# Hybrid five-branch layer: TensorE kept in program order throughout, and the merge of branch D put ahead of that of branch B

## The chip, the cores and the metric

The kernel runs on one core of one Trainium2 chip. The metric is the time on the device in microseconds (us), from which a median over several runs is taken. Each run of the profiler also leaves one traced execution, and all durations below come from that one.

## The reference

One layer over 256 tokens of width 1024. One large projection feeds five branches that read the same input: A causal block attention, B a mixture of three dilated windows, C attention with forgetting, D a gated delta rule, E cross-attention into a memory of 256 tokens. Each branch's output is gated, projected back to width 1024, weighted by a sigmoid gate and summed.

```
h = x @ w_in + b_in                       # every q, k, v, z and merge gate
o_a, o_b, o_c, o_d, o_e                   # 256 x 384 each, 6 heads of 64 (E: 4 of 96)
o = stack(o_a .. o_e) * silu(z)           # (S, 5, 384)
y = einsum('snc,ncd->snd', o, w_branch)   # 5 projections to width 1024
y = sum(sigmoid(merge_logits) * y, axis=n)
return layer_norm(2**0.25 * x + y @ w_out)
```

D needs small serial pieces: a causal convolution of 4 taps on its q, k and v, cumulative sums of log decays, and a triangular solve in chunks of 64.

## The kernel before

**Main stream.** Every large product is made of units. A unit loads 128x1024 of weights (`raw`, 7 buffers), ScalarE rounds them to `hi` and VectorE takes the rest `lo` (helper `split`; 3 buffers each), and TensorE then runs three matmuls for each block of 128 (`mm3`: hi by hi, hi by lo, lo by hi), 24 matmuls of 256 columns for a feature-major unit. `ORDER` is the list of blocks, three or four units each: `dk` is D's key projection, `zc` the gate of C, `merge_b` the merge of branch B (8 times 24 matmuls for the gate and 9 for the projection). A merge block needs its branch's gated output and calls `need("og" + br)` before its projection.

**Side streams.** The branches' own work is written as generators (`scalars`, the convolutions `conv`, `d_front`, `d_base`, `d_levels`, `d_solve`, three `attend`, `cross`, and so on). After each chunk of a unit (9 matmuls as a rule) `stepper` lets up to three of them take a step. In a step a generator issues a few instructions and yields, one or more chunks. All logits of all branches go through one PSUM tile (`lg`, one buffer, helper `lgps`), transposes through two (`tp`), the outputs of the heads through one (`av`).

**What sets the order on an engine.** The program is only the first word on it. The framework's scheduler plays the program against a timeline of its own at compile time and sets a fixed order for each engine; an instruction that is not ready there is passed by others that are. `tc.keep_in_program_order(ins)` takes an instruction out of that freedom with respect to the others marked so. Before, only the last out-projections carry the mark (`keep=not first`). On the chip each engine follows its fixed list.

Names in the lists below: `mm_299`, `mm_370` and `mm_417` are the PSUM tiles of successive units (second and third unit of `dk`, first of `dq`), `fg` the log decays that `scalars` makes from a chain of some twenty small VectorE instructions (L333 to L360), `tp_353` and `tp_357` their cumulative sums (L364 to L369), `grow` a copy of those that goes to DRAM (`gscr`, L376) and comes back broadcast as `gr` (L465, for D) and `mf` (L797, for C; L802 and L803 turn it into masks), `yc` the convolution (L389 to L392), `dconv` its result (L397), which L432 (q and k) and L451 (v) transpose. `lg_4595` and `lg_4599` are logits of the cross-attention (L897), whose exponentials L905 makes before L911 transposes them. L738 to L767 are the softmax of A, B and C (L754 the exponentials on ScalarE), L773 its transposes and L776 their copy, L689 the gating.

Of the kernel before, what the change touches and what calls it, by code (L numbers as in the profile page):

```python
# [29 lines left out]
ORDER = ("dk dq cq dv ck zc av za ak zd aq bq0 bk0 bk2 bq1 merge_a bk1 bv"  # L30
         " merge_c zb bq2 ze eq mk mv merge_b merge_d merge_e").split()
MERGES = [n for n in ORDER if n.startswith("merge")]
# [43 lines left out]
def kernel(ctx: ExitStack, tc: tile.TileContext, T: dict, out: bass.AP):  # L76
# [8 lines left out]

    V_, A_, PE, G_ = nc.vector, nc.scalar, nc.tensor, nc.gpsimd
    uid = [0]

# [36 lines left out]

    def mm3(pt, lh, ll, rh, rl, first, last, keep=False):
        for l, r, start, stop in ((lh, rh, first, False), (lh, rl, False, False), (ll, rh, False, last)):
            ins = PE.matmul(pt, l, r, start=start, stop=stop)  # L128
            if keep:
                tc.keep_in_program_order(ins)  # L130

    def together(*products):

        for pt, l, r, start, stop in products:
            PE.matmul(pt, l, r, start=start, stop=stop)  # L135

# [174 lines left out]
    for _ in range(WARM):  # L311
        PE.matmul(wup[:, 0], zero[:, 0:P], zero, start=True, stop=True)

    def scalars():

        yield from wait("sc")
        nc.sync.dma_start(cst[:, C_MA:], T["cst"][:, C_MA:])
        nc.sync.dma_start(gnw, T["gnw"])
        nc.sync.dma_start(mgb, T["mgb"])
        nc.sync.dma_start(vb, T["vb"].to_broadcast([P, 2, BW]))  # L320

        V_.tensor_scalar(cwh, cw, 0.5, None, op0=ALU.mult)
        hb = bcol[:, 3 * len(FM):]
        V_.tensor_scalar(hb, hb, 0.5, None, op0=ALU.mult)
# [36 lines left out]
        yield  # L361

        pt = tpps((P, 2, 18))
        PE.matmul(pt[:, 0], K(C_TRI), fg[:, 0], start=True, stop=True)  # L364
        PE.matmul(pt[:, 1], K(C_ONE), fg[:, 0], start=True, stop=False)
        PE.matmul(pt[:, 1], K(C_TRI), fg[:, 1], start=False, stop=True)
        p2 = tpps((18, S))
        PE.matmul(p2, fg[:, 0], K(C_TRI, 256), start=True, stop=False)
        PE.matmul(p2[:, P:], fg[:, 1], K(C_TRI), start=False, stop=True)  # L369
        yield  # L370
        V_.tensor_scalar(ngt, pt, -1.0, None, op0=ALU.mult)
        grow = ct("grow", (18, S))
        V_.tensor_copy(grow, p2)
        R["gscr"] = dr.tile([18, S], F32, name="gscr")
        yield
        nc.sync.dma_start(R["gscr"], grow)  # L376
        flag("scalars")
# [45 lines left out]
    def d_front():  # L423
# [3 lines left out]
        for qi, key in ((1, "k"), (0, "q")):  # L427
            yield from wait((key, 2))
            for t in range(2):
                pt = tpps((P, 3, P))  # L430
                for m in range(3):
                    PE.transpose(pt[:, m], dconv[key][:, m, t * P:(t + 1) * P], ident)  # L432
                yield
# [14 lines left out]
        for t in range(2):  # L448
            pt = tpps((P, 6, HD))
            for m in range(3):  # L450
                PE.transpose(pt[:, 2 * m:2 * m + 2], dconv["v"][:, m, t * P:(t + 1) * P], ident)  # L451
            yield
# [103 lines left out]
    def d_levels():  # L556
# [5 lines left out]
        for b in range(4):  # L562
            r = slice(32 * b, 32 * b + 32)
            for g in range(12):
                PE.matmul(y[r, g], AT[r, g, r], Tc[r, g, 0:16], start=True, stop=True)
            yield
# [4 lines left out]
        for b in range(4):  # L571
            r, c = slice(32 * b, 32 * b + 32), 32 * (b % 2)
            for g in range(12):
                PE.matmul(z[32 * b:32 * b + 16, g], ys[r, g, 0:16], Uc[r, g, c + 16:c + 32], start=True, stop=True)
                if b % 2 == 0:
                    PE.matmul(zt[r, g], Uc[r, g, 0:32], ys[r, g, 0:16], start=True, stop=True)
            yield
# [9 lines left out]
        for i, j in ab:  # L587
            for g in range(12):
                PE.matmul(y[j, g], AT[i, g, j], Tc[i, g], start=True, stop=True)
            yield  # L590
# [5 lines left out]
        for i, j in ab:  # L596
            for g in range(12):
                PE.matmul(z[i, g], ys[j, g], Uc[j, g, 32:64], start=True, stop=True)
            yield
# [5 lines left out]
    def d_solve():  # L605
# [5 lines left out]
        def solve(g):  # L611
            hs, hsl = range(3 * g, 3 * g + 3), slice(3 * g, 3 * g + 3)
            for t in range(2):
                if t == 1:
                    pt = tpps((P, 3, HD))
                    for x, h in enumerate(hs):
                        PE.matmul(pt[:, x], AT[:, 12 + h], W[:, 0, h], start=True, stop=True)
                    yield
                    V_.tensor_tensor(V[:, 1, hsl], V[:, 1, hsl], pt, op=ALU.subtract)
                    yield  # L620
                for b in range(2):
                    r = slice(64 * b, 64 * b + 64)
                    if b == 1:
                        pt = tpps((P, 3, HD))
                        for x, h in enumerate(hs):
                            PE.matmul(pt[r, x], AT[0:64, 6 * t + h, r], W[0:64, t, h], start=True, stop=True)
                        yield
# [3 lines left out]
                    for x, h in enumerate(hs):  # L631
                        PE.matmul(pt[r, x], Uc[r, 6 * t + h], V[r, t, h], start=True, stop=True)
                    yield
# [10 lines left out]
        for t in range(2):  # L644
            pt = lg[:, t]
            for h in range(H):
                if t == 0:
                    PE.matmul(pt[:, h], PT[:, h], W[:, 0, h], start=True, stop=True)
                else:
                    PE.matmul(pt[:, h], PT[:, 12 + h], W[:, 0, h], start=True, stop=False)  # L650
                    PE.matmul(pt[:, h], PT[:, 6 + h], W[:, 1, h], start=False, stop=True)
                if h % 2:
# [65 lines left out]
    def attend(br, groups, vname, maskf, width):  # L718
# [5 lines left out]
        def pair(m):  # L724
# [46 lines left out]
            for x in range(2):  # L771
                for i in range(3):
                    PE.transpose(lg[:, x, i * P:(i + 1) * P], L[x][0][:, i * P:(i + 1) * P], ident)  # L773
            yield
# [41 lines left out]
    def mem_norm():  # L816
# [25 lines left out]
        for k in range(KD):  # L842
            pt = tpps((P, S))
            for t in range(2):
                PE.transpose(pt[:, t * P:(t + 1) * P], mr[t][:, k * P:(k + 1) * P], ident)
            yield
# [23 lines left out]
    def token_gate(o, zs, br, scalar=None):  # L870
        dst = R["og" + br] = (f3t(F32R), f3t(F32R))
        for m in range(3):
            pt = tpps((P, S))
            for t in range(2):
                PE.transpose(pt[:, t * P:(t + 1) * P], o[:, t, m * P:(m + 1) * P], ident)
            yield
# [5 lines left out]
    def cross():  # L882
# [5 lines left out]
        def pair(t, g):  # L888
# [4 lines left out]
            for x, h in enumerate(hs):  # L893
                parts = HQ[h]
                for i, (m, a0, a1) in enumerate(parts):
                    krhs = kp if (h == 3) else ke[:, m]
                    PE.matmul(lg[:, x, :S], qe[a0:a1, m, t * P:(t + 1) * P], krhs[a0:a1], start=i == 0, stop=i == len(parts) - 1)  # L897
            yield
# [10 lines left out]
            for pe, pt in zip(pes, (p2[:, 0], p2[:, 1])):  # L909
                for x in range(2):  # L910
                    PE.transpose(pt[:, x], pe[:, x * P:(x + 1) * P], ident)  # L911
            yield
# [5 lines left out]
            for i, h in enumerate(hs):  # L918
                for x in range(2):
                    PE.matmul(avt[t][:, h], pT[:, i, x], ve[:, x, h * 96:(h + 1) * 96], start=x == 0, stop=x == 1)  # L920
            if g == 1:
# [75 lines left out]
    def out_units():  # L997
# [3 lines left out]
        def out_mm(u, k, t, i, first, last):  # L1001
# [5 lines left out]
            else:  # L1007
                h, l = u.h[:, lo:hi], u.l[:, lo:hi]
            mm3(fin["p"][t][i][:, :hi - lo], yh, yl, h, l, first, last, keep=not first)

# [171 lines left out]
```

## Time and profile before

| | |
|---|---|
| median of 3 runs | 498.63 us (498.0 to 501.67) |
| the profiled execution | 500.0 us |
| its span, first to last instruction | 497.9 us |
| TensorE busy | 475.3 us, 95% of the span |
| VectorE busy | 338.1 us, 68% |
| ScalarE busy | 270.3 us, 54% |
| mean granted TensorE clock | 0.964 of full speed |

The time of the profiled execution is 2.1 us more than its span. PE stands for TensorE, DVE for VectorE, ACT for ScalarE, POOL for GpSimd, SP for the queue that issues the loads. A granted clock of 1.00 is 2.4 GHz, 0.50 is 1.2 GHz.

### The profile page before, as it was taken

How to read it: one execution, taken by the hardware profiler on the slowest of the kernel's cores; microseconds unless marked ns; L12 is line 12 of the kernel's file. 1: busy time of each engine (PE TensorE's matmuls, PEld its weight loads, DVE VectorE, ACT ScalarE, POOL GpSimd, SP SyncE). 2: the span in 40 equal slices, each digit the busy share in tenths (PEclk: the TensorE clock that was granted, in tenths of full speed). 3: DMA queues.
4: the chain of work that ended last, by engine and by line, in shares of the span. 5: the costliest groups of instructions: out<-in, count | busy, mean ns of one | idle time of the engine just before them, and what ended most of it. 6: DMA issues, size and time to landing. Idle time of an engine off the chain costs nothing. (4 is left out here: it accounts for less than half of the span.)

```text
span 497.9 us, 10146 instructions
## 1 busy us (share of the span) xinstructions
PE 475.3 (95%) x3957; PEld 442.7 (89%) x3957; DVE 338.1 (68%) x764; ACT 270.3 (54%) x521; POOL 30.7 (6%) x36
## 2 busy tenths in 40 slices
PE   7999999989989999999999999999969999999994
PEld 4999999979978999999999999898737999999973
DVE  4898998876955344669886664866543766678747
ACT  5555684765654233386645566737364555467610
POOL 0000030120000000000001110000001212100000
PEclk9999999999999599999999999999958999999997
DMA  8995676453533123356566874534600566677302
GB/s 262 363 334 179 205 232 216 153 167 102 170 70 109 57 59 118 117 151 189 176 192 200 257 229 139 155 102 127 240 35 0 176 190 183 202 224 232 141 1 84
DMA packets 35052, 81.38 MB, mean 163 GB/s; under 512 B 8971, under 2 KB 17469, under 8 KB 34877
## 3 DMA queue, kind: packets, MB, share of 16 engines
q1 hardware_dynamic: 34715, 80.22, 51.3%
q8 instruction: 31, 0.51, 0.4%
q10 hardware_dynamic: 288, 0.52, 0.3%
q14 instruction: 18, 0.13, 0.1%
HBM read 79.37 MB, written 1.36 MB: 162 GB/s over the span
## 5 line engine op out<-in xcount | busy, mean ns | idle before, releaser
L124 DVE TENSOR_TENSOR lo<-raw,hi 128x1024 fp32r<-128x1024 f32 (+4 forms) x163 | 172.5, 1060 | 88.8 <-ACT hi L123 88.2
L123 ACT ACTIVATE hi<-raw 128x1024 fp32r<-128x1024 f32 (+4 forms) x163 | 146.4, 901 | 139.6 <-PE mm L128 102.8
L128 PE MATMUL mm<-xhi,hi 128*128 128x256 f32 x776 | 221.1, 285 | 0.2
L128 PE MATMUL mm<-xhi,lo 128*128 128x256 f32 x776 | 219.0, 283 | 0.7 <-DVE lo L124 0.7
L128 PE MATMUL mm<-xlo,hi 128*128 128x256 f32 x776 | 218.5, 282 | 0.0
L128 PEld LDWEIGHTS mm<-xhi,lo 128*128 128x128 f32 x776 | 147.7, 191 | 4.1 <-issue 1.4
L128 PEld LDWEIGHTS mm<-xhi,hi 128*128 128x128 f32 x776 | 148.1, 191 | 2.8 <-issue 1.0
L128 PEld LDWEIGHTS mm<-xlo,hi 128*128 128x128 f32 x776 | 148.2, 191 | 0.6 <-issue 0.3
L128 PE MATMUL mm<-f,hi 128*128 128x256 f32 x240 | 45.3, 283 | 0.1
L972 POOL TENSOR_TENSOR yacc<-yacc,yt 128x256 f32<-128x256 f32 x24 | 20.0, 838 | 312.1 <-DVE yt L971 312.1
L128 PEld LDWEIGHTS mm<-f,hi 128*128 128x128 f32 x240 | 36.8, 188 | 1.0 <-ACT f L123 0.5
L128 PE MATMUL mm<-f,lo 128*128 128x256 f32 x120 | 33.7, 282 | 0.0
L128 PEld LDWEIGHTS mm<-f,lo 128*128 128x128 f32 x120 | 22.6, 188 | 0.1
L954 ACT ACTIVATE th<-mm,bcol 128x256 f32<-128x256 f32 x40 | 18.3, 458 | 0.0
L128 PE MATMUL mm<-hi,xhi 128*128 128x384 f32 (+1 forms) x48 | 16.5, 367 | 2.0 <-ACT hi L123 2.0
L128 PE MATMUL mm<-lo,xhi 128*128 128x384 f32 (+1 forms) x48 | 17.5, 364 | 0.4 <-DVE lo L124 0.4
L754 ACT ACTIVATE pr<-pr,mm 128x128 f32<-128x128 f32 (+1 forms) x36 | 15.8, 443 | 3.6 <-DVE mm L745 3.6
L128 PE MATMUL mm<-hi,xlo 128*128 128x384 f32 (+1 forms) x48 | 17.1, 357 | 0.0
L738 DVE CUSTOM_DVE_ANT_0 pr<-lg,cst 128x128 f32<-128x128 f32 (+1 forms) x48 | 14.4, 352 | 4.0 <-PE lg L135 4.0
L135 PE MATMUL lg<-f,f 64*128 64x256 f32 (+1 forms) x144 | 16.9, 351 | 0.0
L971 DVE SCALAR_TENSOR_TENSOR yt<-th,mm 128x256 f32<-128x256 f32 x32 | 13.4, 420 | 3.7 <-PE mm L128 2.8
L480 POOL TENSOR_SCALAR_AFFINE_SELECT pr<-pr 128x256 f32<-128x256 f32 x6 | 9.4, 1576 | 95.3 <-DVE pr L479 91.3
(234 smaller groups left out, 577.1 us busy)
## 6 DMA issues: line engine op xcount, KB each, us to landing
raw<-in_wf_dram SPq DMA_DIRECT2D x60, 512.0 KB, 4.3
raw<-in_wm_dram SPq DMA_DIRECT2D x40, 512.0 KB, 3.7
raw<-in_wb_dram SPq DMA_DIRECT2D x40, 192.0 KB, 2.4
raw<-in_wt_dram SPq DMA_DIRECT2D x12, 384.0 KB, 3.5
raw<-in_wo_dram SPq DMA_DIRECT2D x8, 512.0 KB, 4.7
gr<-gscr SPq DMA_DIRECT2D x12, 128.0 KB, 3.4
raw<-in_wcs_dram SPq DMA_DIRECT2D x3, 402.0 KB, 6.5
raw<-in_mem_dram SPq DMA_DIRECT2D x2, 512.0 KB, 3.4
```

The source lines that it names most:

```text
L123: A_.activation(hi, src, AF.Copy)
L124: V_.tensor_tensor(lo, src, hi.bitcast(F32), op=ALU.subtract)
L128: ins = PE.matmul(pt, l, r, start=start, stop=stop)
L135: PE.matmul(pt, l, r, start=start, stop=stop)
L480: G_.affine_select(E[:, 0::2], E[:, 0::2], pattern=[[0, 2], [1, P]], compare_op=ALU.is_ge, fill=-BIG, base=0, channel_multiplier=-1)
L738: V_.tensor_tensor_reduce(l[:, sl], pts[x][:, sl], mk[x][:, sl], 1.0, 3.0e38, ALU.add, ALU.min, mx[x][:, t, g:g + 1])
L754: A_.activation(l[:, sl], l[:, sl], AF.Exp, bias=mms[x][:, t:t + 1], scale=-1.0, accum_out=sm_[x][:, t, g:g + 1])
L954: A_.activation(th, p, AF.Tanh, bias=bcol[:, i:i + 1], scale=0.5)
L971: V_.scalar_tensor_tensor(yt, st_["th"], 1.0, st_["p"], op0=ALU.add, op1=ALU.mult)
L972: (V_ if last else G_).tensor_tensor(yacc[:, d], yacc[:, d], yt, op=ALU.add)
```

## The change

Two things. The mark that keeps program order is put on every TensorE instruction of the kernel (each matmul and each transpose), so that the scheduler can't move any of them past another. And in `ORDER` the block `merge_d` changes places with `merge_b`. VectorE, ScalarE, GpSimd and the loads are still ordered by the scheduler, which now plays them against a TensorE that waits where its next instruction waits.

```diff
-         " merge_c zb bq2 ze eq mk mv merge_b merge_d merge_e").split()
+         " merge_c zb bq2 ze eq mk mv merge_d merge_b merge_e").split()
...
+    keep = tc.keep_in_program_order
...
-    def mm3(pt, lh, ll, rh, rl, first, last, keep=False):
+    def mm3(pt, lh, ll, rh, rl, first, last):
         for l, r, start, stop in ((lh, rh, first, False), (lh, rl, False, False), (ll, rh, False, last)):
-            ins = PE.matmul(pt, l, r, start=start, stop=stop)
-            if keep:
-                tc.keep_in_program_order(ins)
+            keep(PE.matmul(pt, l, r, start=start, stop=stop))
...
-            PE.matmul(pt, l, r, start=start, stop=stop)
+            keep(PE.matmul(pt, l, r, start=start, stop=stop))
...
-        PE.matmul(pt[:, 0], K(C_TRI), fg[:, 0], start=True, stop=True)
+        keep(PE.matmul(pt[:, 0], K(C_TRI), fg[:, 0], start=True, stop=True))
...
-                    PE.transpose(pt[:, m], dconv[key][:, m, t * P:(t + 1) * P], ident)
+                    keep(PE.transpose(pt[:, m], dconv[key][:, m, t * P:(t + 1) * P], ident))
...
-            mm3(fin["p"][t][i][:, :hi - lo], yh, yl, h, l, first, last, keep=not first)
+            mm3(fin["p"][t][i][:, :hi - lo], yh, yl, h, l, first, last)
```

Line numbers: the change moves the lines from 88 to 125 of the kernel before down by two; from 132 on they agree again.

TensorE's list, third and fourth unit. Before, the second unit of `dk` is followed by the next units:

```order
L128 MATMUL mm_299<-xhi,hi_226 128x256
L128 MATMUL mm_299<-xlo,hi_226 128x256
L128 MATMUL mm_299<-xhi,lo_227 128x256
L128 MATMUL mm_370<-xhi,hi_295 128x256
L128 MATMUL mm_370<-xlo,hi_295 128x256
L128 MATMUL mm_417<-xhi,hi_366 128x256
L128 MATMUL mm_417<-xlo,hi_366 128x256
L128 MATMUL mm_370<-xhi,lo_296 128x256
```

In the changed kernel the cumulative sums of `scalars` stand there:

```order
L130 MATMUL mm_299<-xhi,hi_226 128x256
L130 MATMUL mm_299<-xlo,hi_226 128x256
L130 MATMUL mm_299<-xhi,lo_227 128x256
L364 MATMUL tp_353<-fg,cst 128x18
L365 MATMUL tp_353<-fg,cst 128x18
L366 MATMUL tp_353<-fg,cst 128x18
L368 MATMUL tp_357<-cst,fg 18x256
L369 MATMUL tp_357<-cst,fg 18x128
L130 MATMUL mm_370<-xhi,hi_295 128x256
L130 MATMUL mm_370<-xlo,hi_295 128x256
L130 MATMUL mm_370<-xhi,lo_296 128x256
```

The five products of L364 to L369 have moved from the eleventh unit to between the second and the third, ahead of some 200 matmuls of the main stream.

VectorE's list at the same place. Before, the chain that makes `fg` runs in between the splits and the convolution (`lo_461` is the weight rest for the sixth unit of `dk` and `dq`):

```order
L347 TENSOR_TENSOR s_269<-s_269,e 128x24
L407 MEMSET xp_455 128x3
L392 SCALAR_TENSOR_TENSOR yc_384<-xp_361,cwh,yc_384 128x256
L348 TENSOR_TENSOR s_270<-s_269 128x24
L124 TENSOR_TENSOR lo_461<-raw_293,hi_460 128x1024
L407 MEMSET xp_506 128x3
L349 TENSOR_SCALAR lp<-s_270 128x24
L397 SCALAR_TENSOR_TENSOR f_29_289<-th_345,yc_323 128x256
```

In the changed kernel the chain is finished first, and the masks of C follow it at once:

```order
L359 TENSOR_SCALAR fg<-lp 128x6 x2
L360 TENSOR_TENSOR fg<-lp,fg 128x6 x2
L371 TENSOR_SCALAR ngt<-tp_353 128x36
L373 COPY grow<-tp_357 18x256
L802 SCALAR_TENSOR_TENSOR mf_1101<-mf_1101,ngt,cst 128x128
L803 SCALAR_TENSOR_TENSOR mf_1101<-mf_1101,ngt,cst 128x256
L802 SCALAR_TENSOR_TENSOR mf_1102<-mf_1102,ngt,cst 128x128
L126 TENSOR_TENSOR lo_461<-raw_293,hi_460 128x1024
L389 TENSOR_SCALAR yc_427<-xp_408,cwh 128x256
```

`lo_461` has moved from amid the chain to behind the rest of it and behind three instructions that read `mf`, which comes back from DRAM after L373.

TensorE's list where the cross-attention begins. Before, it stands in a projection of `merge_b` (`f_651` and `f_652` are the two parts of B's gated output, `mm_4882` the projection):

```order
L128 MATMUL mm_4882<-f_651_3895,hi_4836 128x256
L128 MATMUL mm_4882<-f_652_3896,hi_4836 128x256
L128 MATMUL mm_4882<-f_651_3895,lo_4837 128x256
L897 MATMUL lg_4595<-f_734_4347,f_705_4199 128x256 x3
L911 MATMUL tp_4650<-cst,pr_4631 128x128 x2
L897 MATMUL lg_4599<-f_734_4347,f_705_4199 128x256 x2
L897 MATMUL lg_4599<-kp_4442,f_705_4199 128x256
L911 MATMUL tp_4650<-cst,pr_4633 128x128 x2
L920 MATMUL av_4678<-f_779_4572,pT_4663 128x96 x4
```

In the changed kernel it stands in the first unit of `merge_d`, with main matmuls behind it:

```order
L130 MATMUL mm_4581<-xhi,lo_4551 128x256
L897 MATMUL lg_4595<-f_734_4347,f_705_4199 128x256 x3
L897 MATMUL lg_4599<-f_734_4347,f_705_4199 128x256 x2
L897 MATMUL lg_4599<-kp_4442,f_705_4199 128x256
L130 MATMUL mm_4581<-xhi,hi_4550 128x256
L130 MATMUL mm_4581<-xlo,hi_4550 128x256
```

The first transposes (L911), which stood between the two sets of logits, have moved behind 24 main matmuls, and the second set follows the first directly.

## Rows read from the trace of the kernel before

**Rows 1.** The page: busy time by engine, and the clock in 40 slices.

```profile
PE 475.3 (95%) x3957; PEld 442.7 (89%) x3957; DVE 338.1 (68%) x764; ACT 270.3 (54%) x521; POOL 30.7 (6%) x36
...
PEclk9999999999999599999999999999958999999997
```

**Rows 2.** Stretches: busy time and count by engine, granted clock, DMA share, GB/s.

```profile
24.40:64.90 40.50, 40.50 (x343) 39.31 (x342) 37.13 (x99) 24.12 (x44) 0.87 (x2) 1.00 0.71 235
64.90:104.90 40.00, 40.00 (x316) 37.68 (x314) 35.62 (x89) 26.30 (x52) 8.26 (x4) 1.00 0.58 191
104.90:140.00 35.10, 33.33 (x288) 30.11 (x287) 27.12 (x89) 22.00 (x46) 1.32 (x3) 1.00 0.49 143
140.00:158.00 18.00, 16.11 (x206) 14.36 (x205) 8.05 (x25) 8.84 (x22) 0.00 (x0) 0.91 0.44 118
158.00:175.00 17.00, 17.00 (x203) 15.68 (x199) 7.33 (x18) 5.95 (x14) 0.00 (x0) 0.70 0.13 43
175.00:310.00 135.00, 135.00 (x1228) 131.52 (x1227) 86.18 (x159) 73.87 (x126) 6.81 (x8) 1.00 0.56 168
310.00:354.00 44.00, 42.74 (x331) 38.41 (x329) 28.66 (x80) 28.39 (x67) 0.00 (x0) 1.00 0.48 159
354.00:390.00 36.00, 29.85 (x166) 22.39 (x167) 17.51 (x48) 17.44 (x56) 3.42 (x3) 0.81 0.16 52
```

**Rows 3.** Chain that ended last, in order of time: start us, us, what.

```profile
360.77 5.36 ACT pr L754 x24
366.13 0.46 ACT pr L905 x2
...
366.64 0.69 PE tp L911 x2
```

**Rows 4.** TensorE's timeline: first matmuls of two units (48 apart), and L364 to L369.

```profile
24.10 0.28 PE L128 MATMUL mm<-xhi,hi 128*128 128x256 f32 x1
...
29.76 0.28 PE L128 MATMUL mm<-xhi,hi 128*128 128x256 f32 x1
...
48.72 0.26 PE L364 MATMUL tp<-fg,cst 128*128 128x18 f32 x1
...
49.80 0.38 PE L369 MATMUL tp<-cst,fg 128*18 128x128 f32 x2
```

**Rows 5.** VectorE's timeline: the third split, the chain of `scalars`, the copy, the mask.

```profile
25.33 1.23 DVE L124 TENSOR_TENSOR lo<-raw,hi 128x1024 fp32r<-128x1024 f32 x1 [0.74 <-ACT hi L123]
...
29.04 0.18 DVE L348 TENSOR_TENSOR s<-s 128x24 f32<-128x24 f32 x1
...
45.23 0.23 DVE L360 TENSOR_TENSOR fg<-lp,fg 128x6 f32<-128x6 f32 x2
...
50.85 0.41 DVE L373 COPY grow<-tp 18x256 f32<-18x256 f32 x1
...
60.43 0.34 DVE L802 SCALAR_TENSOR_TENSOR mf<-mf,ngt,cst 128x128 f32<-128x128 f32 x1
```

**Rows 6.** The queue of loads (SP): issue of `grow` to DRAM and of its two readers.

```profile
51.28 0.36 SPq L376 DMA_DIRECT2D gscr<-grow  x1
53.57 2.04 SPq L465 DMA_DIRECT2D gr<-gscr  x4
...
56.13 1.86 SPq L797 DMA_DIRECT2D mf<-gscr  x4
```

**Rows 7.** Groups by line and shape: count, busy us, mean ns, idle before.

```profile
L124 DVE TENSOR_TENSOR lo<-raw,hi 128x1024 fp32r<-128x1024 f32 x106 | 134.7, 1272 | 56.8 <-ACT hi L123 56.2 <-PE mm L128 0.2
...
L392 DVE SCALAR_TENSOR_TENSOR yc<-xp,cwh,yc 128x256 f32<-128x256 f32 x18 | 8.3, 476 | 0.1
...
L776 ACT ACTIVATE pT<-lg 128x768 f32<-128x768 f32 x9 | 7.3, 808 | 13.2 <-PE lg L773 13.1
...
L500 DVE SCALAR_TENSOR_TENSOR big<-lg,cj,pr 128x256 f32<-128x256 f32 x12 | 5.7, 477 | 0.0
...
L738 DVE CUSTOM_DVE_ANT_0 pr<-lg,mf 128x256 f32<-128x256 f32 x6 | 2.5, 419 | 0.0
```

More of the change, by code (lines that the diff above doesn't have):

```diff
@@ L311 @@
     for _ in range(WARM):
-        PE.matmul(wup[:, 0], zero[:, 0:P], zero, start=True, stop=True)
+        keep(PE.matmul(wup[:, 0], zero[:, 0:P], zero, start=True, stop=True))
     def scalars():
@@ L363, in scalars @@
         pt = tpps((P, 2, 18))
-        PE.matmul(pt[:, 0], K(C_TRI), fg[:, 0], start=True, stop=True)
-        PE.matmul(pt[:, 1], K(C_ONE), fg[:, 0], start=True, stop=False)
-        PE.matmul(pt[:, 1], K(C_TRI), fg[:, 1], start=False, stop=True)
+        keep(PE.matmul(pt[:, 0], K(C_TRI), fg[:, 0], start=True, stop=True))
+        keep(PE.matmul(pt[:, 1], K(C_ONE), fg[:, 0], start=True, stop=False))
+        keep(PE.matmul(pt[:, 1], K(C_TRI), fg[:, 1], start=False, stop=True))
         p2 = tpps((18, S))
-        PE.matmul(p2, fg[:, 0], K(C_TRI, 256), start=True, stop=False)
-        PE.matmul(p2[:, P:], fg[:, 1], K(C_TRI), start=False, stop=True)
+        keep(PE.matmul(p2, fg[:, 0], K(C_TRI, 256), start=True, stop=False))
+        keep(PE.matmul(p2[:, P:], fg[:, 1], K(C_TRI), start=False, stop=True))
         yield
@@ L450, in d_front @@
             for m in range(3):
-                PE.transpose(pt[:, 2 * m:2 * m + 2], dconv["v"][:, m, t * P:(t + 1) * P], ident)
+                keep(PE.transpose(pt[:, 2 * m:2 * m + 2], dconv["v"][:, m, t * P:(t + 1) * P], ident))
             yield
@@ L564, in d_levels @@
             for g in range(12):
-                PE.matmul(y[r, g], AT[r, g, r], Tc[r, g, 0:16], start=True, stop=True)
+                keep(PE.matmul(y[r, g], AT[r, g, r], Tc[r, g, 0:16], start=True, stop=True))
             yield
@@ L573, in d_levels @@
             for g in range(12):
-                PE.matmul(z[32 * b:32 * b + 16, g], ys[r, g, 0:16], Uc[r, g, c + 16:c + 32], start=True, stop=True)
+                keep(PE.matmul(z[32 * b:32 * b + 16, g], ys[r, g, 0:16], Uc[r, g, c + 16:c + 32], start=True, stop=True))
                 if b % 2 == 0:
-                    PE.matmul(zt[r, g], Uc[r, g, 0:32], ys[r, g, 0:16], start=True, stop=True)
+                    keep(PE.matmul(zt[r, g], Uc[r, g, 0:32], ys[r, g, 0:16], start=True, stop=True))
             yield
@@ L588, in d_levels @@
             for g in range(12):
-                PE.matmul(y[j, g], AT[i, g, j], Tc[i, g], start=True, stop=True)
+                keep(PE.matmul(y[j, g], AT[i, g, j], Tc[i, g], start=True, stop=True))
             yield
@@ L597, in d_levels @@
             for g in range(12):
-                PE.matmul(z[i, g], ys[j, g], Uc[j, g, 32:64], start=True, stop=True)
+                keep(PE.matmul(z[i, g], ys[j, g], Uc[j, g, 32:64], start=True, stop=True))
             yield
@@ L616, in solve @@
                     for x, h in enumerate(hs):
-                        PE.matmul(pt[:, x], AT[:, 12 + h], W[:, 0, h], start=True, stop=True)
+                        keep(PE.matmul(pt[:, x], AT[:, 12 + h], W[:, 0, h], start=True, stop=True))
                     yield
@@ L625, in solve @@
                         for x, h in enumerate(hs):
-                            PE.matmul(pt[r, x], AT[0:64, 6 * t + h, r], W[0:64, t, h], start=True, stop=True)
+                            keep(PE.matmul(pt[r, x], AT[0:64, 6 * t + h, r], W[0:64, t, h], start=True, stop=True))
                         yield
@@ L631, in solve @@
                     for x, h in enumerate(hs):
-                        PE.matmul(pt[r, x], Uc[r, 6 * t + h], V[r, t, h], start=True, stop=True)
+                        keep(PE.matmul(pt[r, x], Uc[r, 6 * t + h], V[r, t, h], start=True, stop=True))
                     yield
@@ L647, in d_solve @@
                 if t == 0:
-                    PE.matmul(pt[:, h], PT[:, h], W[:, 0, h], start=True, stop=True)
+                    keep(PE.matmul(pt[:, h], PT[:, h], W[:, 0, h], start=True, stop=True))
                 else:
-                    PE.matmul(pt[:, h], PT[:, 12 + h], W[:, 0, h], start=True, stop=False)
-                    PE.matmul(pt[:, h], PT[:, 6 + h], W[:, 1, h], start=False, stop=True)
+                    keep(PE.matmul(pt[:, h], PT[:, 12 + h], W[:, 0, h], start=True, stop=False))
+                    keep(PE.matmul(pt[:, h], PT[:, 6 + h], W[:, 1, h], start=False, stop=True))
                 if h % 2:
@@ L772, in pair @@
                 for i in range(3):
-                    PE.transpose(lg[:, x, i * P:(i + 1) * P], L[x][0][:, i * P:(i + 1) * P], ident)
+                    keep(PE.transpose(lg[:, x, i * P:(i + 1) * P], L[x][0][:, i * P:(i + 1) * P], ident))
             yield
@@ L844, in mem_norm @@
             for t in range(2):
-                PE.transpose(pt[:, t * P:(t + 1) * P], mr[t][:, k * P:(k + 1) * P], ident)
+                keep(PE.transpose(pt[:, t * P:(t + 1) * P], mr[t][:, k * P:(k + 1) * P], ident))
             yield
@@ L874, in token_gate @@
             for t in range(2):
-                PE.transpose(pt[:, t * P:(t + 1) * P], o[:, t, m * P:(m + 1) * P], ident)
+                keep(PE.transpose(pt[:, t * P:(t + 1) * P], o[:, t, m * P:(m + 1) * P], ident))
             yield
@@ L896, in pair @@
                     krhs = kp if (h == 3) else ke[:, m]
-                    PE.matmul(lg[:, x, :S], qe[a0:a1, m, t * P:(t + 1) * P], krhs[a0:a1], start=i == 0, stop=i == len(parts) - 1)
+                    keep(PE.matmul(lg[:, x, :S], qe[a0:a1, m, t * P:(t + 1) * P], krhs[a0:a1], start=i == 0, stop=i == len(parts) - 1))
             yield
@@ L910, in pair @@
                 for x in range(2):
-                    PE.transpose(pt[:, x], pe[:, x * P:(x + 1) * P], ident)
+                    keep(PE.transpose(pt[:, x], pe[:, x * P:(x + 1) * P], ident))
             yield
@@ L919, in pair @@
                 for x in range(2):
-                    PE.matmul(avt[t][:, h], pT[:, i, x], ve[:, x, h * 96:(h + 1) * 96], start=x == 0, stop=x == 1)
+                    keep(PE.matmul(avt[t][:, h], pT[:, i, x], ve[:, x, h * 96:(h + 1) * 96], start=x == 0, stop=x == 1))
             if g == 1:
```

## The prediction

> **What bounds the kernel now.** I read the page first, then busy time by stretches, then the timelines and the queue of loads around the places where the order changes. The page [rows 1] shows TensorE busy for 475.3 us of a span of 497.9, which is 95%; VectorE has 68%. So TensorE's list is the kernel, and the time is its work plus every gap in it. The stretches [rows 2] say where gaps are: none from 24.4 to 104.9 and from 175 to 310 (busy time equals length), 1.77 us in 104.9 to 140, 1.89 in 140 to 158, 1.26 in 310 to 354, 6.15 in 354 to 390. The same rows show what the throttle costs: a granted clock of 0.91 over 18 us is 1.6 us, 0.70 over 17 us is 5.1. In 354 to 390 the mean of 0.81 amounts to 13.7 us at the lower level (36 x 0.19 / 0.5); at most 6.15 of those fall in idle time, so some 7.5 us of work ran at half speed and cost 3.75. The chain of waits [rows 3] shows what opened that hole: 24 entries of another branch's exponentials, 5.36 us in a row on ScalarE, ahead of the one that the cross-attention's transposes needed.
>
> Two things follow. All that a better order can win behind 104.9 us is 11.1 us of idle time and 10.4 of clock, 21.5 together. And ahead of 104.9 us TensorE never waits, so every wait that a fixed order puts there is added to the end in full. VectorE is busy for 37.13 of 40.5 us there [rows 2], so it has little to catch up with.
>
> **Front, first wait.** The cumulative sums L364 to L369 now stand behind the second unit. TensorE gets there when it began its third unit before, at 24.10 [rows 4]. They need `fg`. On VectorE the list up to L348 has not got shorter: the third split runs at 25.33 and L348 at 29.04 [rows 5]. Then come some 20 small operations of the chain, now without others between them; at about 0.12 us from start to start for such sizes, an estimate from their 0.18 to 0.23 us in those rows with overlap, that is 2.5 us. So `fg` is there at 31.6 and TensorE **waits 7.5 us**. Before, `fg` was ready at 45.5 and used at 48.72 [rows 4, 5], so nobody waited. The low end is 4, if the chain squeezes in beside the splits; the high end is 12, if VectorE's splits get in between.
>
> **Front, second wait.** The five products take 1.5 us (48.72 to 50.2 [rows 4]), say 1.3 to the last start, and the next two units 5.7 us (24.10 to 29.76 [rows 4], 0.118 a matmul). So at 38.6 TensorE stands before the transposes of `k` (L432), which need the third slice of its convolution. On VectorE that slice now waits behind masks that read `mf`. Worked out: `fg` at 31.6, products to 32.9, the copy `grow` some 1.1 us behind (50.2 to 51.26 [rows 4, 5]), 34. From the issue of `grow` to the mask it took 9.15 us (51.28 to 60.43 [rows 5, 6]; on the way 2.3 us until the readers could be issued, 2.04 of issues for `gr`, 4.3 from the issue of `mf` to the mask). So the first mask starts at 43, and VectorE, which takes its list in order, stands still meanwhile with a weight split (`lo_461`) behind it. Behind the first mask come about 19 operations up to L397: two splits of 1.27, five masks and nine convolution steps at 0.35 to 0.48, and the product [rows 7]; 9.8 us by means, and I take 8 since neighbours overlap. The slice is there at 51 and TensorE **waits 12.4 us**. Bounds: 6, if the round trip through DRAM takes half with less traffic, and 16 if a split more gets ahead. This wait ends at VectorE's time, not TensorE's: whatever TensorE loses ahead of it, a lower clock after the first wait included, is swallowed by it.
>
> **Front, smaller waits.** The transposes of `q` stand 24 matmuls, 2.8 us, behind the unit that they need, and those of `v` 33 matmuls, 3.9 us. The chain between is two ScalarE steps, four steps of convolution and a product, at no more than 0.48 each, and two or three splits of 1.27 in between [rows 7]: about 7 us. So **4 us each** (for `v` a square root on ScalarE comes on top); ends 0 and 6. The front adds 7.5 + 12.4 + 4 + 4 = **28**.
>
> **Clock in the front.** The trace shows that a wait of 6 us at 360 to 371 was followed by work at half speed, 3.75 us lost [rows 2]. The second wait is twice as long: I add **3.75**; after the first it is swallowed, after the shorter ones I take none (rival below). The Trainium skill, page "TensorE: Matmul & The Clock Gate", section "HAM oscillation — how this bites in real kernels", says that idle gaps of TensorE throttle it and that warming up is paid for again after each; the 0.81 of this trace agrees, and the 1.00 of the stretch before 140 shows that small gaps do not.
>
> **Middle.** With a single `lg` buffer, products that stand back to back wait for its reader. For C two sets of logits stand so (four L738 of 0.42 at most, 1.4 with overlap), two sets of transposes (the copy L776, 0.81) and later readers like L500 at 0.48, four of them [rows 7]: 4.2. For A I take 2.5 of the same kind, its softmax standing further from its logits. **7**, ends 0 and 10. B's logits stand 9 matmuls apart, 1.06 us, against 1.4 for L738, a wait of 0.34 at six places: 2; the solve of D and the transposes of the memory 1. **3**, ends 0 and 6.
>
> **Late, with the swap.** The hole of 354 to 390 cost 6.15 + 3.75. `merge_d` ahead of `merge_b` puts D's 264 matmuls there, which need nothing of B: 31 us of cover by 0.118. But ScalarE's list still has exponentials ahead of the one that reads `lg_4595`, and `lg_4599` follows directly and needs the same buffer: TensorE, which can't go round it, waits some 6 us (5.36 + 0.46 [rows 3]) with the cover behind it. Net **0**; ends −9.9 and +8.
>
> **Gains.** D's chain begins earlier by some 140 instructions in TensorE's list, so the gaps of 1.77 and 1.89 and the first clock dip of 1.6 may go: **−5**. What is late next there is the split of weights. The dip at 158 to 175 has no idle time; it is the solve's small products, and these stay.
>
> **Sum.** 500.0 + 28 + 3.75 + 7 + 3 + 0 − 5 = 536.75 for an execution like the profiled one. That stood 1.4 us above the median of its runs, so **535**.
>
> **Rivals.** *The clock falls after every wait:* the ones at `q` and `v` and three in the middle lose 3.75 each as well: 535 + 19 = 554. For it speaks the hole at 360, against it the clock of 1.00 in 104.9 to 140 beside 1.77 us of idle time [rows 2]. The section of the Trainium skill's page "TensorE: Matmul & The Clock Gate" named above would have it so; by it the time would be this 554. *The gains pay for the front:* only the two large waits come (20), all else is covered and all of the 21.5 comes back: 498.5 − 1.4, **497**, no change. For it speaks that side work stands earlier everywhere; against it that 5.1 of the 21.5 are the solve's own clock. *Faster:* the price of the front is the time that `fg` and then `mf` take to come. If both come at the low ends, waits of 4 and 6, and all else goes as in the rival before, 500 + 10 − 21.5 − 1.4 = **487**. It decides at a front of 16: below that, with every gain, the kernel is over 1% faster. Against it stand VectorE's 37.13 busy of 40.5 us and the 9.15 us of the trip, each measured. *That the order does not change* is out: the lists show the moved rows.
>
> **How the numbers follow.** Forecast 0.73 (518 to 548 by its own bounds, since not all terms err one way), clock after every wait 0.15, no change 0.07, faster 0.05. The range takes in the forecast and most of the first rival and leaves out the last two: 510 to 556. Within 1%, about what a measurement of this kernel can tell from no change: 0.07. Faster 0.05, slower 0.88.
>
> **What would show it.** In the changed profile: TensorE idle ahead of L364 from about 24 to 32, released by VectorE's L360; a second and longer wait ahead of L432 that ends near 51, while VectorE itself waits at L802 for the DMA of `mf`; digits of the clock at 5 in the third to fifth slice; shorter waits ahead of L432 (second set) and L451; waits ahead of L135 for L738 and L776; and ahead of the second L897 a wait for L905 on ScalarE. Busy time of TensorE should be 475 plus what a lower clock adds. The prediction is wrong if the wait at L364 is under 3 us, if VectorE's mask does not wait for `mf`, or if idle time behind 104.9 us falls to nothing.

## The result and the profile after

The changed kernel takes 548.4 us (median of 4 runs, 545.44 to 549.31) against 498.31 for the kernel before, 1.0988 times as long, 95% interval 1.0913 to 1.1062. Forecast were 535 us, with a range of 510 to 556. A run over 1.5% longer than the fastest of its kernel counts as slow and the ratios use fast runs alone; in experiment 5 two of the four runs were slow, the profiled one among them.

The page of the changed kernel, busy time and clock in 40 slices [rows 1]:

```profile
PE 485.2 (89%) x3957; PEld 451.1 (83%) x3957; DVE 342.4 (63%) x764; ACT 271.6 (50%) x521; POOL 23.8 (4%) x36
...
PEclk9966898999999998999999999999968899999998
```

Its span is 546.2 us, 48.3 more than before. TensorE's busy time grew by 9.9 us with the same 3957 instructions, so 38.4 us are new idle time and 9.9 are instructions that took longer. The digits of the clock are down in four slices of the first fifth, in one behind it and at three quarters.

To see where the 48.3 us arise, I count the matmuls of the main line (L128 before, L130 after) from the start up to a time at which both kernels have done the same number (count behind PE busy). Before:

```profile
0.00:72.70 72.70, 63.14 (x469) 59.74 (x470) 0.98 0.77 259
...
0.00:277.60 277.60, 226.31 (x1681) 212.32 (x1682) 0.97 0.56 174
0.00:398.20 398.20, 312.62 (x2353) 293.93 (x2354) 0.96 0.53 165
```

After:

```profile
0.00:107.90 107.90, 68.47 (x466) 65.48 (x467) 0.84 0.55 182
...
0.00:317.20 317.20, 230.21 (x1683) 217.39 (x1684) 0.93 0.49 153
0.00:446.50 446.50, 321.48 (x2354) 302.93 (x2355) 0.93 0.47 147
```

Some 467 matmuls are done 35.2 us later than before, 1682 are 39.6 later, 2354 are 48.3 later. So the front costs 35, what lies between it and 317 us some 4, and what follows some 9.

TensorE's waits by releaser (total us, times, longest):

```profile
PE tp L432 <- DVE xp L407: 11.6, 2, 8.5
PE tp L364 <- DVE fg L360: 8.5, 1, 8.5
PE lg L135 <- DVE mx L738: 5.9, 4, 2.5
PE tp L451 <- DVE f L397: 5.2, 3, 2.1
PE lg L897 <- ACT pr L905: 4.5, 1, 4.5
```

Of these, the trace before has only a wait of the cross-attention for L905, at L911. The largest stand in the front. TensorE's timeline there (start, us, and in brackets the idle time ahead of it):

```profile
33.35 0.61 PE L364 MATMUL tp<-fg,cst 128*128 128x18 f32 x2 [8.53 <-DVE fg L360]
...
43.05 0.38 PE L432 MATMUL tp<-cst,f 128*128 128x128 f32 x2
51.91 0.47 PE L432 MATMUL tp<-cst,f 128*128 128x128 f32 x1 [8.48 <-DVE xp L407]
...
65.89 0.33 PE L432 MATMUL tp<-cst,f 128*128 128x128 f32 x1 [3.09 <-DVE xp L407]
```

VectorE's in the same stretch [rows 5]:

```profile
30.00 0.18 DVE L348 TENSOR_TENSOR s<-s 128x24 f32<-128x24 f32 x1
...
33.13 0.29 DVE L360 TENSOR_TENSOR fg<-lp,fg 128x6 f32<-128x6 f32 x2
...
43.31 0.35 DVE L802 SCALAR_TENSOR_TENSOR mf<-mf,ngt,cst 128x128 f32<-128x128 f32 x1 [6.64 <-DMA mf<-gscr]
...
51.43 0.42 DVE L397 SCALAR_TENSOR_TENSOR f<-th,yc 128x256 f32<-128x256 f32 x1
```

The queue of loads [rows 6]:

```profile
36.69 0.36 SPq L376 DMA_DIRECT2D gscr<-grow  x1
...
39.89 1.86 SPq L797 DMA_DIRECT2D mf<-gscr  x4
```

This is the chain of the forecast. `fg` ends at 33.4 and TensorE has waited 8.53 us for it. The copy `grow` goes out at 36.69, VectorE stands still for 6.64 us until `mf` is back and masks from 43.31 on, and the third slice of `k` is finished at 51.85. Its transpose starts at 51.91, after the second wait of 8.48 us. (The rows name L407 as what released it, the short VectorE instruction behind L397.)

The clock after the waits, in stretches that follow them (columns: length, busy us and count of PE, PEld, DVE, ACT and POOL, granted clock, DMA share, GB/s):

```profile
34.00:39.00 5.00, 5.00 (x21) 4.01 (x22) 0.61 (x2) 0.00 (x0) 0.00 (x0) 0.50 0.02 4
...
52.00:56.00 4.00, 4.00 (x19) 4.00 (x20) 0.98 (x2) 0.52 (x2) 0.00 (x0) 0.50 0.00 0
...
66.00:70.00 4.00, 3.70 (x18) 3.51 (x19) 2.44 (x6) 0.50 (x2) 0.95 (x2) 0.57 0.43 137
...
92.00:97.00 5.00, 4.99 (x24) 4.99 (x25) 1.11 (x2) 0.80 (x1) 0.00 (x0) 0.50 0.08 32
...
405.00:411.00 6.00, 6.00 (x22) 4.64 (x21) 1.07 (x3) 2.32 (x7) 0.00 (x0) 0.50 0.01 2
420.00:428.00 8.00, 8.00 (x26) 5.63 (x27) 3.33 (x4) 2.57 (x8) 0.72 (x1) 0.58 0.26 85
```

TensorE is busy nearly all through these stretches, at 1.2 GHz in most of each. A wait is followed by 3 to 7 us of work at half speed, also the one of 3.09 us at 65.89 and the three of 1.7, 2.1 and 1.4 us at 86 to 92.

### The profile page after: what moved, and what is told of

Same layout as the page of the kernel before. It is cut to its first block, busy times and chain, and to the rows that moved or that the text cites. A ratio compares the mean times of both kernels' runs of the same rounds, so it can differ in the third digit from the quotient of the medians.

```text
span 546.2 us, 10155 instructions
## 1 busy us (share of the span) xinstructions
PE 485.2 (89%) x3957; PEld 451.1 (83%) x3957; DVE 342.4 (63%) x764; ACT 271.6 (50%) x521; POOL 23.8 (4%) x36
## 5 line engine op out<-in xcount | busy, mean ns | idle before, releaser
L130 PE MATMUL mm<-xhi,hi 128*128 128x256 f32 x776 | 228.3, 294 | 0.0
L130 PE MATMUL mm<-xlo,hi 128*128 128x256 f32 x776 | 220.7, 284 | 0.0
L130 PE MATMUL mm<-xhi,lo 128*128 128x256 f32 x776 | 220.3, 284 | 0.2 <-DVE lo L126 0.2
L130 PEld LDWEIGHTS mm<-xhi,hi 128*128 128x128 f32 x776 | 152.1, 196 | 5.9 <-issue 4.2
L130 PEld LDWEIGHTS mm<-xlo,hi 128*128 128x128 f32 x776 | 151.7, 195 | 0.2
L130 PEld LDWEIGHTS mm<-xhi,lo 128*128 128x128 f32 x776 | 151.2, 195 | 0.4 <-DVE lo L126 0.4
L130 PE MATMUL mm<-f,hi 128*128 128x256 f32 x240 | 45.7, 286 | 0.0
L130 PEld LDWEIGHTS mm<-f,hi 128*128 128x128 f32 x240 | 37.4, 192 | 0.3 <-issue 0.3
L130 PE MATMUL mm<-f,lo 128*128 128x256 f32 x120 | 34.2, 285 | 0.0
L972 POOL TENSOR_TENSOR yacc<-yacc,yt 128x256 f32<-128x256 f32 x24 | 18.7, 779 | 338.4 <-DVE yt L971 338.4
L130 PEld LDWEIGHTS mm<-f,lo 128*128 128x128 f32 x120 | 23.0, 192 | 0.0
L135 PEld LDWEIGHTS lg<-f,f 64*128 64x128 f32 x144 | 10.0, 186 | 12.5 <-DVE mx L738 7.6
L130 PE MATMUL mm<-hi,xhi 128*128 128x384 f32 (+1 forms) x48 | 17.9, 374 | 2.0 <-ACT hi L125 2.0
L738 DVE CUSTOM_DVE_ANT_0 pr<-lg,cst 128x128 f32<-128x128 f32 (+1 forms) x48 | 14.3, 352 | 8.0 <-PE lg L135 8.0
L130 PE MATMUL mm<-lo,xhi 128*128 128x384 f32 (+1 forms) x48 | 17.2, 359 | 0.9 <-DVE lo L126 0.7
L754 ACT ACTIVATE pr<-pr,mm 128x128 f32<-128x128 f32 (+1 forms) x36 | 15.9, 444 | 3.9 <-DVE mm L745 3.9
L971 DVE SCALAR_TENSOR_TENSOR yt<-th,mm 128x256 f32<-128x256 f32 x32 | 13.5, 421 | 5.8 <-PE mm L130 5.0
L130 PE MATMUL mm<-hi,xlo 128*128 128x384 f32 (+1 forms) x48 | 17.0, 354 | 0.0
```

The source lines that it names most:

```text
L130: keep(PE.matmul(pt, l, r, start=start, stop=stop))
L135: keep(PE.matmul(pt, l, r, start=start, stop=stop))
L738: V_.tensor_tensor_reduce(l[:, sl], pts[x][:, sl], mk[x][:, sl], 1.0, 3.0e38, ALU.add, ALU.min, mx[x][:, t, g:g + 1])
L754: A_.activation(l[:, sl], l[:, sl], AF.Exp, bias=mms[x][:, t:t + 1], scale=-1.0, accum_out=sm_[x][:, t, g:g + 1])
L971: V_.scalar_tensor_tensor(yt, st_["th"], 1.0, st_["p"], op0=ALU.add, op1=ALU.mult)
L972: (V_ if last else G_).tensor_tensor(yacc[:, d], yacc[:, d], yt, op=ALU.add)
```

## The experiments

Eleven kernels. "After" is the changed kernel, "lag" the time by which a number of main matmuls is done later than in another kernel, counted as above.

**1. The swap alone.** Kernel before with

```diff
-         " merge_c zb bq2 ze eq mk mv merge_b merge_d merge_e").split()
+         " merge_c zb bq2 ze eq mk mv merge_d merge_b merge_e").split()
```

> The kernel before with the two merge blocks exchanged and no new mark. If the waits of the changed kernel come from the fixed order and the swap by itself is neutral: 498 us, within 1% of before. If the loss of some 8 us that the changed kernel shows behind 354 us is the swap's: 503 to 508.

Measured 489.3 us, ratio 0.9803 (0.9759 to 0.9846): some 2% faster, and the whole interval lies below 1, which neither case had. The hole of 354 to 390 us is gone [rows 2]:

```profile
354.00:390.00 36.00, 35.20 (x266) 30.25 (x264) 23.02 (x56) 21.36 (x58) 5.62 (x6) 1.00 0.44 139
```

35.20 of 36 us are busy, at a clock of 1.00. ScalarE's exponentials stand as they did [rows 3], here from 363.22 on, ahead of L905:

```profile
363.22 0.40 ACT L754 ACTIVATE pr<-pr,mm 128x128 f32<-128x128 f32 x1 [2.69 <-DVE mm L745]
...
370.21 0.46 ACT L905 ACTIVATE pr<-lg,mxe 128x256 f32<-128x256 f32 x1
```

Through them TensorE now runs main matmuls, and the first transposes and second logits come when they are ready, with no idle time ahead:

```profile
371.56 0.38 PE L911 MATMUL tp<-cst,pr 128*128 128x128 f32 x2
371.88 1.32 PE L897 MATMUL lg<-f,f 64*128 64x256 f32 x4
```

So the swap did supply cover, and a free TensorE uses it. Set against this kernel, the marks cost not 50 us but 59.

The counterpart is the changed kernel with the two blocks in their old order, the marks alone (run `keep_noswap`):

```diff
-         " merge_c zb bq2 ze eq mk mv merge_d merge_b merge_e").split()
+         " merge_c zb bq2 ze eq mk mv merge_b merge_d merge_e").split()
```

Expected were 545 to 552 us if a TensorE in fixed order can't use the cover, and 555 to 560 if the swap brings it the same 9 us as the free kernel. Measured 549.88 us, 1.1044 (1.0993 to 1.1096), which can't be told from the 548.4 of the changed kernel. The wait of 4.5 us at the second logits is there too:

```profile
PE lg L897 <- ACT pr L905: 6.3, 2, 4.5
```

So the swap is worth 9 us to a free TensorE and nothing that shows to one in fixed order.

**2. The mark by kind of matmul.** The mark on the side products alone:

```diff
+    def mm3(pt, lh, ll, rh, rl, first, last, mark=False):
...
+            ins = PE.matmul(pt, l, r, start=start, stop=stop)
+            if mark:
+                keep(ins)
```

> The changed kernel with the mark taken from the matmuls of the main stream (helper mm3, other than those of before), so that only the products of the side streams are held in order. Its list has the sums L364 to L369 back behind the tenth unit. Theory that a fixed place of the side products makes the front wait: 525 to 548. Rival, that it is the mark on the main matmuls, which then can't pass a product that isn't ready: no wait of over 1 us ahead of 100 us, 498 to 510.

Measured 489.7 us, 0.9832 (0.9782 to 0.9882), the same as the swap without marks. The rival had the cause right (no wait of over 1 us between the start-up and 100 us) and the time too high. That the marks cost nothing here is a net result: C's transposes wait 4.3 us for L776 (L778 there), and the lower clock of 140 to 178 us is gone, 1.00 against 0.82 before. In turn the mark on the main matmuls alone (`keep(...)` taken off every other product):

> The changed kernel with the mark on the main matmuls alone (mm3); the side products are free. Its list still has the sums between the second and the third unit, the masks on VectorE ahead of the third slice of the convolution. If the mark on the main matmuls is what costs: both large waits at the front are there, 8 us each, 540 to 550. If the mark on the side products costs: 498 to 515.

Measured 535.85 us, 1.0764 (1.0705 to 1.0822): 46.6 us above the swap alone, of the 59.1 that all marks cost. Its largest waits:

```profile
PE tp L432 <- DVE xp L407: 10.6, 2, 7.6
PE lg L135 <- DVE mx L738: 7.3, 4, 3.2
PE lg L135 <- DVE f L397: 4.8, 1, 4.8
PE tp L911 <- ACT pr L905: 4.0, 1, 4.0
```

The second wait of the front, the softmax's and the cross-attention's are all there with the side products free; only the first one is short (2.1 us), because a product of D has gone ahead of the sums and waits there instead (4.8 us for L397). So the side products need no mark to stand too early: once the main matmuls hold their order, the scheduler puts the sums between the second and third unit by itself, and only where the main matmuls are free do these pass them.

**3. The sums later.** All marked; `scalars` waits for q's last slice before it issues the sums:

```diff
+        yield from wait(("q", 2))
...
         pt = tpps((P, 2, 18))
```

> The changed kernel, all marked, but the stream of the scalars waits for the last slice of q before it issues the sums, which then stand 130 matmuls later, with the masks of C behind the convolutions of k and q on VectorE. If the front's loss is the place of the sums (8.5 us of wait at L364 and 8.5 at L432, and the clock): both gone, shorter waits of 2 to 4 us left at the transposes, 523 to 532. If TensorE would only wait elsewhere instead, for the splits or the convolutions: 540 to 550.

Measured 536.14 us, 1.075 (1.0702 to 1.0799), 12 less than after and between the two cases. Both large waits are gone, but L432 (L433 there) waits 8.1 us in four places and L451 (L452 there) 6.2. The lag over before at 504 main matmuls is some 25 us where after has 35, so the gain in the front is 10.

**4. The masks later.** All marked; on VectorE the convolution's product and the masks hold program order too:

```diff
-            V_.scalar_tensor_tensor(mf[:, 0:P], ...)
+            keep(V_.scalar_tensor_tensor(mf[:, 0:P], ...))
...
-            V_.scalar_tensor_tensor(dconv[key][:, m], th, 1.0, y, op0=ALU.add, op1=ALU.mult)
+            keep(V_.scalar_tensor_tensor(dconv[key][:, m], th, 1.0, y, op0=ALU.add, op1=ALU.mult))
```

> The changed kernel, with the products of the convolutions (L397) and the masks of C (L802, L803) on VectorE also held in program order, so that the masks stand behind all nine slices of the convolution; the sums stay where they are. If the second wait at the front, 8.5 us at L432, is the masks' round trip through DRAM: that wait falls under 3 us, VectorE no longer waits 6.6 us for mf, and the time is 533 to 541. If another thing on VectorE (splits, convolutions) is as late: the wait stays over 5 us, 543 to 550.

Measured 546.4 us, 1.0927 (1.0856 to 1.0999), which can't be told from after. TensorE's timeline:

```profile
31.41 0.61 PE L364 MATMUL tp<-fg,cst 128*128 128x18 f32 x2 [8.23 <-DVE fg L360]
...
45.49 0.47 PE L432 MATMUL tp<-cst,f 128*128 128x128 f32 x1 [3.64 <-DVE f L397]
...
60.22 0.33 PE L432 MATMUL tp<-cst,f 128*128 128x128 f32 x1 [3.09 <-DVE xp L407]
```

VectorE no longer waits for `mf`, and the second wait fell from 8.48 to 3.64 us. The rest of it is not the masks: the third unit of `dk` stands behind the sums (its last matmul starts at 38.53), and its convolution, which begins at 41.01, can't begin before that unit is done. The lag at 504 matmuls is 30 us instead of 35. But at 648 it is 49, against 50 in after. Most of the 5 us was lost again behind C's first logits: both kernels wait there for 2.49 us, but here the work behind that wait ran at half speed and in after at full speed (lines in the last section).

**5. The whole front later.** All marked; the sums as in 3 and eight, eight and six more steps ahead of the transposes:

```diff
             yield from wait((key, 2))
+            for _ in range(8): yield
...
         yield from wait("scalars", ("v", 2))
+        for _ in range(6): yield
```

> The changed kernel, all marked, but in the program the sums stand behind q's last slice and the transposes of k, q and v eight, eight and six steps later. If the 35 us that are lost by 108 us are products that stand too early, not the fixed order as such: no wait over 2 us ahead of 105 us, 512 to 522. If a fixed order loses them to whatever comes next (splits, C's logits): 530 to 545.

Measured 545.14 us, 1.0852 (1.0775 to 1.0928). Its four runs took 538.66, 543.43, 546.85 and 547.36 us, and the profile is of the longest. Its waits:

```profile
PE lg L775 <- DVE big L503: 7.0, 2, 4.0
PE lg L135 <- DVE mx L740: 5.7, 4, 2.3
PE tp L364 <- DVE fg L360: 4.7, 1, 4.7
PE lg L899 <- ACT pr L907: 4.5, 1, 4.5
```

The front alone came near what was expected: the lag at 504 matmuls is 12 us instead of 35, though two waits of over 2 us were left ahead of 105 us. One is that of the sums, which wait for `fg` again (4.7 us at 45.81), as VectorE finishes it later as well (L360 at 45.59, against 33.13 in after); the other is that of C's first logits for the softmax (2.3 us at 95.53). At 648 matmuls the lag is 41, against 50 in after: C's transposes and logits wait for L501 (L503 there). How much of this its shorter runs have is not shown. After from 24.4 to 104.9 us, busy PE, PEld, DVE, ACT and POOL:

```profile
24.40:104.90 80.50, 54.92 (x393) 52.14 (x392) 49.38 (x122) 32.36 (x56) 3.01 (x4) 0.81 0.45 143
```

This kernel:

```profile
24.40:104.90 80.50, 69.68 (x512) 65.46 (x510) 62.26 (x171) 43.72 (x84) 2.55 (x5) 0.92 0.57 177
```

Before, VectorE was busy for 72.75 us there (37.13 + 35.62 [rows 2]). It did 23.4 us less of its work in that stretch in the changed kernel and 10.5 less in this one. It is TensorE's supplier for D and C behind it. That what it had not done there made the later waits is a reading that fits their releasers; no run separates it.

**6. The marks by stage.** The swap, and marks on TensorE in one part of the program only; `now` is the unit, `first[...]` a block's first unit:

```diff
+    def keep(ins):
+        if first["zc"] <= now[0] < first["merge_d"]:
+            tc.keep_in_program_order(ins)
```

for the middle; up to `zc` for the front, from `merge_d` on for the late part.

> The changed kernel with the marks on TensorE only up to the block zc (the sums, the transposes of k and q, the first 15 units); behind it TensorE is free as before. TensorE's list is that of the changed kernel up to the transposes of v. If each stage costs what its waits and its lower clock cost there: 489 (the swap alone) plus 30 to 35, 519 to 525. If a free TensorE behind it makes good what VectorE did not get done: 495 to 512.

> The changed kernel with the marks from the block zc up to merge_d, free ahead of it and behind. By the waits of the softmax, D's chain and v: 489 plus 6 to 12, 495 to 501. If its waits are only the late front's consequence: 487 to 491.

> The changed kernel with the marks from merge_d on alone (merge_d, merge_b, merge_e and the side products that stand among them, the cross-attention above all). If the fixed order takes back the cover that the swap gives: 489 plus 15 to 19, 504 to 508, with a wait of 4 us ahead of the second set of L897's logits. If the late loss of the changed kernel is a consequence of being late in the front: 487 to 492.

Measured against the swap's 489.3 us: front 516.1 (+26.8), middle 513.1 (+23.8), late 503.4 (+14.1). The three sum to 64.7, and all marks together cost 59.1. So each stage pays by itself. The front has a lag of some 33 us over the swap at 504 matmuls and has 26 at 1080, after D's solve. Its list is not quite that of the changed kernel, as its expectation has it: a product of D, which has no mark there, stands ahead of the sums and waits 4.8 us for L397 (L406 there), as in the run with main matmuls alone marked. The middle, expected at 6 to 12, comes to C's first logits at 89.68 us, where the changed kernel came at 118.46. It has two waits for L501 (L510 there) that the changed kernel had not, 4.57 and 1.81 us:

```profile
74.35 1.65 PE L144 MATMUL lg<-f,f 64*128 64x256 f32 x8 [4.57 <-DVE big L510]
...
89.68 0.93 PE L144 MATMUL lg<-f,f 64*128 64x128 f32 x8 [2.50 <-DVE mx L747]
...
101.17 0.88 PE L782 MATMUL lg<-cst,pr 128*128 128x128 f32 x6 [1.81 <-DVE big L510]
```

Its lag over the swap is 25 us at 648 matmuls, 11.7 at 1800 and 22 at the end. Of these last 10 us the trace shows 5.4 in five waits for B's softmax (310 to 354 us), 1.8 in a wait for a split on ScalarE at 380 and 1.6 in work at half speed behind it (380.7 to 384). In the late part the second logits wait with main matmuls behind them, and the clock is at 0.50 from 352.6 to 369.6 us:

```profile
355.20 3.52 PE L906 MATMUL lg<-f,f 96*128 96x256 f32 x6 [1.30 <-DVE mx L747]
361.57 2.37 PE L906 MATMUL lg<-f,f 64*128 64x256 f32 x4 [2.85 <-ACT pr L914]
```

**7. D's products marked.** The swap and the mark on L560 to L651 alone (eleven `keep(...)`).

> The kernel before with the merge blocks exchanged and the mark on the products of D's solve and its output alone (L560 to L651). In the run with the marks on all side products the stretch from 140 to 178 us was 7 us shorter than before, its clock 1.00 instead of 0.89, while the softmax of C lost some 10 us ahead of it. If those 7 us come from D's products standing together: 481 to 486. If they were only the 10 us given back: 488 to 492.

Measured 487.76 us, 0.9781 (0.975 to 0.9813), against 0.9803 for the swap alone: not to be told apart. The clock dip of 158 to 175 us [rows 2] is gone from that stretch,

```profile
158.00:175.00 17.00, 17.00 (x263) 14.86 (x261) 9.81 (x27) 7.44 (x17) 0.00 (x0) 1.00 0.15 47
```

but over 140 to 200 us the clock is 0.94 instead of 0.89 (the stretch that the 0.89 of the expectation belongs to), so about half of the loss is still there, now from 148 to 155 us.

## Why the prediction was right, and where its sizes were off

**What bounds the kernel** was right: waits put into the front were added to the end. By stage the sum forecast 31.75 us for the front, 5 for the middle with its gains and 0 for the late part, 36.75 together. The span grew by 48.3. Measured by the prediction's own terms were 35, 11 (4 up to 317 us and 7 in B's softmax behind it) and 1 to 2. Its signs of being wrong did not come: the wait at L364 was 8.53 us, the mask waited 6.64 for `mf`, and idle time behind 104.9 us grew.

**First wait**: 7.5 forecast, 8.53 measured. `fg` ended 1.8 us later than worked out: L348 stood at 30.00 instead of 29.04, and the small operations took 3.4 us instead of 2.5.

**Second wait**: 12.4 forecast, 8.48 measured, and the difference is not its end (51 forecast, 51.9 measured) but TensorE's arrival, 43.4 instead of 38.6: the first wait ended 1.8 us later, and 5.7 us of work behind it ran at half speed. That loss was swallowed, as the prediction has it. Masks at 43 forecast, 43.31 measured. Experiment 4 shows that the masks make some 5 us of this wait and the sums ahead of the third unit the rest, which the prediction did not separate.

**Smaller waits**: 4 each; 3.4 at q, 5.2 at v.

**Clock in the front**: a term that was mis-sized. Forecast were 3.75 us after the second wait and none after the shorter ones. The stretches show work at half speed behind all of them: 4 us at 52, most of 3.7 at 66 and 5 at 92, half of each lost, some 6 us. With the idle time of 25.6 and the 3 us behind the first wait this is the 35. The price of 3.75 was read from the kernel before as that of a wait of 6 us; the longest single wait there was 3.97 us, and the clock fell within it:

```profile
363.10:376.70 13.60, 9.38 (x33) 7.06 (x34) 4.79 (x15) 6.60 (x25) 0.00 (x0) 0.50 0.00 0
```

So 9.38 us of work ran at half speed there, and 4.7 were lost. The Trainium skill, page "TensorE: Matmul & The Clock Gate", section "HAM oscillation — how this bites in real kernels", has the warming up paid for again after each long idle gap of TensorE. In the front this trace bears that out and goes further: waits of 3.09 us, and three of 1.4 to 2.1 us close together, were followed by half speed as well, where the prediction took them as free. Behind the front some waits of 1.3 to 2.5 us left the clock at 1.00 (last section).

**Middle**: up to 317 us the net came out nearly as said, 4 us against 5, but both sides were larger, so that this is in part luck. The waits of C, D and A (L738, L689, L776, L754, L501) add up to 10.7 us where 7 were forecast, and work at half speed at 134 us costs 1.7 more. Against that, 3.9 us of idle time that the kernel before had from 104.9 to 335 us are gone, and its work at half speed shrank from 13.5 us (148 to 151, 162 to 172) to 6.8 (203 to 210), which gives 3.4 back. Experiment 6 shows that with an undisturbed front the same marks would cost 24.

**B's softmax**: the term that missed by most. Forecast were 2 us, 0.34 at six places, all for L738. TensorE's waits from 330 to 396 us:

```profile
PE lg L773 <- DVE pr L767: 3.5, 3, 1.6
PE lg L135 <- DVE mx L738: 3.4, 3, 1.4
```

These are 6.9 us at six places: three waits for L738 of 0.6 to 1.4 us, and three of 0.9 to 1.6 at the transposes for L767, which the forecast had for C but not for B.

**Late**: net 0 was forecast, and what is left when B's waits are taken out is 1 to 2 us. The wait was right in kind and place, 4.47 us at the second logits for L905 on ScalarE. The forecast had no sum for the clock behind it: 6.6 us of work at 404 and 6.7 at 421 at half speed cost another 6.7. The hole of the kernel before, 6.15 us of idle time and 4.7 of clock, was nearly as dear, so the zero is in part luck. And the reference was too low: the swap gives a free TensorE 9 us there, which the fixed order takes back (experiment 1).

**Which marks**: the prediction did not ask. The expectation ahead of experiment 2 had the side products as its theory, and that was wrong: the mark on the main matmuls alone gives nearly all of the front's lag (33 of 35 us at 504 matmuls) and 46.6 of the 59.1 us in all. **The rivals**: the clock after every wait was right for the front's short waits and wrong for most of those behind; it explains some 2 to 3 of the 11.5 us that the sum was short, B's softmax some 5. Of the gains on which the other two rivals rest, 21.5 us, some 7 came.

What stays open: why the scheduler plans the sums as ready where they are not. Its own timeline was not looked at; that it takes VectorE to be faster than it is would fit the `fg` that is late again in experiment 5, but that is argued, not shown. Nor is it shown why the main and the side marks together cost 12 us more than their costs alone add up to (46.6 and nothing).

## What to carry to other kernels

This engine, 95% busy, lost by a fixed order where a small product that wasn't ready stood ahead of bulk work: the wait of a small product is hidden only as long as bulk work may pass it. So it was the bulk that had to stay free, and marks on small products alone cost nothing net. Moving such products later by hand brought 10 us in the front in one kernel and 23 in the other, but of the 59 us in all only 12 and some 3 to 10 (experiment 5 differs by 9 us from run to run): other products waited in their place, and the supplier's list shifted too. And a block placed as cover (the swap, 2% faster) worked only with an order that could use it.

## What the runs showed of the hardware

Short waits differ in what the clock does behind them. In the changed kernel it stayed at 1.00 in the stretches of 2 us behind single waits of 2.49 us at 118, 1.31 at 368, 1.56 at 382 and 1.44 at 392. It fell to 0.50 behind one of 2.66 us at 134, one of 3.09 at 66, and behind the second of three of 1.4 to 2.1 us at 86 to 92.

The length of the wait does not settle it. The wait of 2.49 us ahead of C's first logits is there in the changed kernel and in experiments 3 and 4. The 6 us behind it in the changed kernel:

```profile
118.46:124.46 6.00, 6.00 (x39) 5.25 (x40) 5.74 (x26) 4.45 (x16) 0.41 (x1) 1.00 0.37 128
```

In experiment 4 (experiment 3 has 0.50 as well, from 108 to 114 us):

```profile
113.50:119.50 6.00, 6.00 (x22) 4.91 (x24) 5.50 (x26) 3.67 (x16) 0.41 (x1) 0.50 0.39 128
```

The same list of products gets through 39 matmuls in the one and 22 in the other. What decides between them is not shown.

The lower clock costs only where it falls on work. In the three long waits of the changed kernel it was at 0.50 while TensorE still stood (28.8 to 33.3, 45.9 to 51.9 and 400.9 to 404.3 us), and 4 to 7 us of work at half speed followed each.
